# Two-layer encoder trunk: where the norms' squares products, the operand sums of the seven-product tiles and the last gate columns stand in the program's order

## The chip, the cores and the metric

The kernel runs on one core of one Trainium2 chip. The metric is the device time of one execution in microseconds (us). The kernel before the change took 2275.96 us in the median of three runs (2275.76 to 2279.22).

## The reference

One inference step of an encoder with two layers, for 1024 prompt frames and 32 sample frames (1056 columns in all, "T"), with a model width of 1024. Layer 0 mixes frames with a matrix-memory recurrence (mLSTM, 8 heads), layer 1 with windowed attention (16 query heads on 2 shared key and value heads). Behind each mixer stands a norm, then a gated feed-forward network (FFN) of width 2816, then another norm:

```
def layer_norm(x, g, b):
    mu = jnp.mean(x, -1, keepdims=True)
    var = jnp.mean(jnp.square(x - mu), -1, keepdims=True)
    return (x - mu) * lax.rsqrt(var + LN_EPS) * g + b

def swiglu(x, w_gu, w_down):
    g, u = jnp.split(x @ w_gu, 2, axis=-1)
    return (jax.nn.silu(g) * u) @ w_down

def trunk(x, ...):
    for layer in range(DEPTH):                 # DEPTH = 2
        if layer < N_A_LAYERS:                 # N_A_LAYERS = 1
            mix, C, n, m = mlstm_mixer(x, ...)
        else:
            k_sh, v_sh = x @ w_kv              # shared keys and values
            mix = swa_prompt(x, k_sh, v_sh, ...)
        x = layer_norm(DEEPNORM_ALPHA * x + mix, ln_g[layer, 0], ln_b[layer, 0])
        x = layer_norm(DEEPNORM_ALPHA * x + swiglu(x, w_gu[layer], w_down[layer]), ln_g[layer, 1], ln_b[layer, 1])
```

So there are four norms. They are numbered 0 (behind the mLSTM), 1 (behind the first FFN), 2 (behind attention) and 3 (behind the second FFN, the output).

## The kernel before

**Precision and products.** All is fp32. TensorE takes each operand as a high and a low half, and one "step" is three products: high by high (L358), high by low (L359), low by high (L360), in `gemm`. For weights, `Weights` loads a raw block `wr` (SyncE), ScalarE casts the high half `wh` (L198), and GpSimd or VectorE makes the low half `wl` (L200, raw minus high); some of these halves lie in borrowed buffers called `ex`. For activations the halves lie in `sx`.

**What sets the order.** The program is written out in one order by a planner, `Weave`. A task is a Python generator; each number that it yields is a span of planned TensorE time. After each step of three products `gemm` calls `tick` with the planned length of that step (0.34 for 264 columns), and tasks whose span has run out issue their next piece there. `drain` runs a task to its end, or until a condition holds, at once. Each engine works off its instructions in the order in which they were issued, so a piece that is issued earlier stands ahead of everything issued later on its engine, ready or not.

**A norm.** Columns are worked on in four quarters of 264. While the projection ahead of a norm makes its eight output tiles for a quarter (for norms 0 and 2 in `mixer_out`, L1098 adds the residual; for norm 1 in the down projection, L1466 does), `norm_tail` adds up the tiles (L595 and L597, VectorE). Then it launches `ln_task` for that quarter, which runs while TensorE goes on with the next quarter or with what follows the norm. Its pieces: the mean's product on TensorE (L417); centring in four instructions (L422, VectorE); the squares on ScalarE (L424); their additions (L426, two instructions on VectorE or GpSimd, and L429, VectorE); then, `yield y[3]` after L429 was issued, the squares product `pv` on TensorE (L433); the reciprocal root on ScalarE and VectorE (L437 to L443); the scaling (L447, VectorE), gain and bias (L457 on ScalarE, L455 on VectorE), the high half (L463) and the low half (L469) of the result. `y` comes from the table `LN_PACE`.

**The FFN.** The 22 pairs of a gate and an up tile (128 rows each) are made one after the other. The first two (`FIRST = 2`) are plain (`up_plain`): one set for the column half c = 0 (quarters 0 and 1), then the same for c = 1 (quarters 2 and 3), whose fourth quarter waits for the fourth `ln_task`. The other 20 take a scheme with seven products of half-size blocks in place of eight (`up_tile`), with four extra operands t1 to t4, which are sums of blocks of the activations. `sums(c)` makes them for one column half: per operand and pair of rows, an addition or subtraction on VectorE (L1248 for t3, L1250 for t2, L1252 for t4, L1254 for t1), the high half on ScalarE (L1238), the low half on VectorE or GpSimd in turn (L1235), one operand per 2.6 planned us; t1 waits until the plain tiles of that half are through. `sums(0)` is launched behind the first three quarters' norm tasks, `sums(1)` behind the fourth's. Before the first seven-product tile, `summed` drains both where they are not done. L1216 is the plain tiles' gating on VectorE.

**Behind norm 1** come the key and value projections of layer 1 (`k_group`, `v_group`), the queries (`q_group`: ScalarE copies at L1541 and L1542, low halves on VectorE at L1543 and L1546), and the attention, which starts with the scores' product (L1630) and its reader on VectorE (L1636).

**Gates.** In layer 0 the mLSTM's gates are worked out per group of 384, 384 and 288 frames by `gate_task`; `gates` makes them (L766 among its last rows is ScalarE's exponential), `gate_columns` transposes three pieces on TensorE (L781), each copied out of PSUM by ScalarE (L782, two PSUM banks in turn), and after the third group a small product brings the decays into columns (L793). `yield 3.0` stands between the third group's gates and its columns.

Of the kernel before, what the change touches and what calls it, by code (L numbers as in the profile page):

```python
# [52 lines left out]
    ((4.0, 1.2, 1.0, 3.6, 1.0, 1.4, 0.9), (3.8, 0.7, 0.8, 4.2, 0.8, 1.4, 1.0)),  # L53
    ((4.2, 0.9, 1.1, 4.4, 1.0, 1.4, 0.8), (4.2, 0.7, 0.9, 4.2, 0.8, 1.4, 0.8)),
)

RUSH = (3.2, 0.8, 0.6, 2.8, 0.8, 1.0, 0.6)

# [3 lines left out]
N4 = T // 4  # L62
# [176 lines left out]
def kernel(ctx: ExitStack, tc: tile.TileContext, A, O):  # L239
# [155 lines left out]

    QUARTERS = [(group(g), (g % 2, slice(0, N4))) for g in range(4)]

    def ln_task(z_, lps, grp, li, last, final):
        cols, (c, zs) = grp
        w = cols.stop - cols.start  # L400

        rush = final and grp is QUARTERS[2]
        y = RUSH if rush else LN_PACE[li & 1][last]
        acc = z_[:, 0:2, c, zs]
        sq = [acc] + [z_[:, 2 + 2 * i : 4 + 2 * i, c, zs] for i in range(3)]
        rs, r2 = z_[:, 8, c, zs], z_[:, 9, c, zs]
        n = KT // 2

        def z2(kk):
            return ACT[:, 2 * kk : 2 * kk + 2, cols]  # L410

        def s2(i, kk):
            return SX[:, i, 2 * kk : 2 * kk + 2, cols]

        yield y[0]
        pm = new(lps, "ln", [P, 512], bufs=3 if li & 1 else 2)[:, :w]
        nc.tensor.matmul(pm, onesm[:], acc[:, 0, :], start=True, stop=True)  # L417
        yield y[1]
        for s in range(n + 2):
            if s < n:  # L420

                nc.vector.tensor_sub(z2(s), pm.unsqueeze(1).broadcast_to([P, 2, w]), z2(s))  # L422
            if 1 <= s <= n:
                nc.scalar.activation(sq[s - 1], z2(s - 1), AF.Square)  # L424
            if s >= 3:
                (nc.gpsimd if rush or not (last or s & 1) else nc.vector).tensor_add(acc, acc, sq[s - 2])  # L426
            yield y[2]
        if not rush:
            nc.vector.tensor_add(acc[:, 0], acc[:, 0], acc[:, 1])  # L429
        yield y[3]  # L430
        pv = new(lps, "ln", [P, 512], bufs=3 if li & 1 else 2)[:, :w]
        for i in range(1 + rush):
            nc.tensor.matmul(pv, onesm[:], acc[:, i, :], start=(i == 0), stop=(i == rush))  # L433
        yield y[4]

        if not li & 1:
            nc.scalar.preload_act_table_set("natural_log_exp_and_others")  # L437
        nc.scalar.activation(rs, pv, AF.Ln, bias=eps_ln[:])
        nc.scalar.activation(rs, rs, AF.Exp, scale=-0.5)
        nc.scalar.activation(r2, rs, AF.Square, scale=0.5 ** 0.5)  # L440
        yield y[5]
        nc.vector.scalar_tensor_tensor(r2, pv, eps_ln[:], r2, op0=ALU.add, op1=ALU.mult)
        nc.vector.scalar_tensor_tensor(rs, r2, 1.5, rs, op0=ALU.subtract, op1=ALU.mult)  # L443
        for s in range(n + 3):
            if s < n:
                eng = nc.gpsimd if rush and s & 1 else nc.vector
                eng.tensor_mul(z2(s), z2(s), rs.unsqueeze(1).broadcast_to([P, 2, w]))  # L447
            kk = s - 1
            if 0 <= kk < n:
                for k in (2 * kk, 2 * kk + 1):  # L450
                    z, gk, bk = ACT[:, k, cols], lng[:, li, k : k + 1], lnb[:, li, k : k + 1]
                    if rush and k & 1:
                        nc.gpsimd.tensor_scalar(z, z, gk, bk, op0=ALU.mult, op1=ALU.add)
                    elif li & 1 and last and k & 1:
                        nc.vector.tensor_scalar(z, z, gk, bk, op0=ALU.mult, op1=ALU.add)  # L455
                    else:
                        nc.scalar.activation(z, z, AF.Identity, scale=gk, bias=bk)  # L457
            kk = s - 2
            if 0 <= kk < n:
                if final:  # L460
                    nc.sync.dma_start(O["y"][:, 2 * kk : 2 * kk + 2, cols], z2(kk))
                else:
                    nc.scalar.copy(s2(0, kk), z2(kk))  # L463
                    if li == 1:
                        nc.scalar.dma_start(scr[:, 2 * kk : 2 * kk + 2, cols], z2(kk))
            kk = s - 3
            if kk >= 0 and not final:
                eng = nc.gpsimd if kk & 1 else nc.vector
                eng.tensor_sub(s2(1, kk), z2(kk), s2(0, kk).bitcast(F32))  # L469
            yield y[6]  # L470
# [186 lines left out]
    cols = [pa.tile([P, 3, 96], F32, name=f"cols{g}") for g in range(3)]  # L657
# [126 lines left out]
    def gate_task():  # L784
        for g in range(3):
            while mst["v"] < 3 * g + 3:
                yield 0.5
            yield from gates(g)
        yield 3.0
        gate_columns(*late.pop())  # L790
        pd = new(psa, "T", [P, 512], bufs=2)
        for j in range(PAIRS):
            nc.tensor.matmul(pd[:, 9 * j : 9 * j + 9], sel[:, j, :], dec[:], start=True, stop=True)  # L793
        nc.vector.tensor_copy(dcol[:], pd[:, : 9 * PAIRS].rearrange("p (j c) -> p j c", j=PAIRS))
# [318 lines left out]
    def ffn(layer, li, tasks, lx, final):  # L1113
# [107 lines left out]
        def sums(c):  # L1221


            def x(k, par):
                return ACT[:, k : k + 2, group(2 * c + par)]

            todo = [(o, k) for k in range(0, H, 2) for o in ("t3", "t2", "t4")] + [("t1", k) for k in range(0, H, 2)]
            bufs = [Z[:, i : i + 2, c, :] for i in (7, 9)]

            def halve(s, low):  # L1230
                if 0 <= s < len(todo):
                    o, k = todo[s]
                    d = X[o](c)[:, :, k : k + 2, :]
                    if low:
                        (nc.vector if s & 1 else nc.gpsimd).tensor_sub(d[:, 1], bufs[s % 2], d[:, 0].bitcast(F32))  # L1235
                        made.append((c, o))
                    else:
                        nc.scalar.copy(d[:, 0], bufs[s % 2])  # L1238

            for s in range(len(todo) + 2):  # L1240
                halve(s - 2, True)
                if s < len(todo):
                    o, k = todo[s]
                    while o == "t1" and not plain[c]:
                        yield 0.3
                    t, before = bufs[s % 2], bufs[(s - 1) % 2]
                    if o == "t3":
                        nc.vector.tensor_sub(t, x(k + H, 1), x(k, 1))  # L1248
                    elif o == "t2":
                        nc.vector.tensor_add(t, before, x(k, 0))  # L1250
                    elif o == "t4":
                        nc.vector.tensor_sub(t, x(k + H, 0), before)  # L1252
                    else:
                        nc.vector.tensor_sub(t, x(k, 1), x(k, 0))  # L1254
                halve(s - 1, False)
                yield 2.6
# [650 lines left out]
```

## Time and profile before

| what | us |
|---|---|
| median of three runs | 2275.96 |
| lowest, highest run | 2275.76, 2279.22 |
| profiled execution, first to last instruction (span) | 2273.4 |
| TensorE busy, of that span | 2196.6 |
| VectorE busy | 1475.9 |
| ScalarE busy | 1013.4 |
| GpSimd busy | 1131.3 |
| mean granted clock of TensorE | 0.990 |

The profiled execution is a single one; what is known of it is its span of 2273.4 us, which is 2.6 us less than the median of the runs. Engines are written PE (TensorE), DVE (VectorE), ACT (ScalarE), POOL (GpSimd) and SP (SyncE, whose queue issues the transfers). A row of a timeline reads: start, duration, engine, line of the program, operation, output and inputs by their names, shapes, number of instructions in the row, and in brackets the idle time of the engine ahead of it with what ended that. L200 is line 200 of the program before; in the changed program the same lines stand 2 to 7 further down (L200 becomes L202, L358 to L360 become L360 to L362, L422, L426, L429 and L433 become L426, L430, L433 and L437, L442 and L447 become L447 and L452, L595 and L597 become L600 and L602, L781 and L793 become L786 and L798, L1098 becomes L1103, L1216 becomes L1221, L1235 and L1238 become L1242 and L1245, L1248, L1250 and L1252 become L1255, L1257 and L1259).

### The profile page before, as it was taken

How to read it: one execution, taken by the hardware profiler on the slowest of the kernel's cores; microseconds unless marked ns; L12 is line 12 of the kernel's file. 1: busy time of each engine (PE TensorE's matmuls, PEld its weight loads, DVE VectorE, ACT ScalarE, POOL GpSimd, SP SyncE). 2: the span in 40 equal slices, each digit the busy share in tenths (PEclk: the TensorE clock that was granted, in tenths of full speed). 3: DMA queues.
4: the chain of work that ended last, by engine and by line, in shares of the span. 5: the costliest groups of instructions: out<-in, count | busy, mean ns of one | idle time of the engine just before them, and what ended most of it. 6: DMA issues, size and time to landing. Idle time of an engine off the chain costs nothing. (4 is left out here: it accounts for less than half of the span.)

```text
span 2273.4 us, 44264 instructions
## 1 busy us (share of the span) xinstructions
PE 2196.6 (97%) x17166; PEld 2152.2 (95%) x17166; DVE 1475.9 (65%) x2771; ACT 1013.4 (45%) x2281; POOL 1131.3 (50%) x1040
## 2 busy tenths in 40 slices
PE   8999999999999999999998999999999999999997
PEld 8889989999999999999998998889999999999997
DVE  4354466777666665466667779877666666466657
ACT  3343355455434444322246788656444444421124
POOL 2443333226666666554326776633666666554422
PEclk9999999999999999999999999999999999999998
DMA  4221212302444434697524211411344344397712
GB/s 147 69 57 52 56 42 71 118 21 73 143 152 152 152 134 151 206 329 245 162 77 139 85 60 44 142 57 47 119 146 142 136 150 161 123 337 252 250 54 77
DMA packets 167298, 291.54 MB, mean 128 GB/s; under 512 B 16496, under 2 KB 123048, under 8 KB 167088
## 3 DMA queue, kind: packets, MB, share of 16 engines
q1 hardware_dynamic: 162736, 284.38, 37.5%
q10 hardware_dynamic: 4352, 4.33, 0.5%
q8 instruction: 135, 2.21, 0.4%
q14 instruction: 75, 0.61, 0.1%
HBM read 203.89 MB, written 82.94 MB: 126 GB/s over the span
## 5 line engine op out<-in xcount | busy, mean ns | idle before, releaser
L200 POOL TENSOR_TENSOR wl_s<-wr,wh_s 128x512 fp32r<-128x512 f32 x224 | 316.5, 1433 | 237.9 <-ACT wh_s L198 166.8
L358 PE MATMUL d<-sx,wh 128*128 128x264 f32 (+2 forms) x1068 | 342.3, 320 | 9.6 <-ACT sx L388 7.5
L360 PE MATMUL d<-sx,wl 128*128 128x264 f32 (+2 forms) x1068 | 327.8, 307 | 2.9 <-DVE wl L200 2.2
L359 PE MATMUL d<-sx,wh 128*128 128x264 f32 (+2 forms) x1068 | 327.7, 307 | 0.5 <-DVE sx L389 0.3
L198 ACT CAST wh_s<-wr 128x512 fp32r<-128x512 f32 x224 | 135.4, 617 | 316.3 <-DVE wr L175 288.6
L358 PE MATMUL A<-sx,wh_s 128*128 128x264 f32 x896 | 254.6, 284 | 2.7 <-ACT z L1299 2.7
L359 PE MATMUL A<-sx,wh_s 128*128 128x264 f32 x896 | 254.2, 284 | 0.0
L360 PE MATMUL A<-sx,wl_s 128*128 128x264 f32 x896 | 254.0, 283 | 0.0
L200 POOL TENSOR_TENSOR wl<-wr,wh 128x512 fp32r<-128x512 f32 (+2 forms) x103 | 141.1, 1376 | 220.8 <-ACT wh L198 190.3
L358 PEld LDWEIGHTS d<-sx,wh 128*128 128x128 f32 x1068 | 204.2, 191 | 14.5 <-ACT sx L388 7.8
L360 PEld LDWEIGHTS d<-sx,wl 128*128 128x128 f32 x1068 | 203.8, 191 | 3.9 <-DVE wl L200 2.8
L359 PEld LDWEIGHTS d<-sx,wh 128*128 128x128 f32 x1068 | 204.6, 192 | 2.0 <-DVE sx L389 1.0
L200 POOL TENSOR_TENSOR wl_a<-wr,wh_a 128x512 fp32r<-128x512 f32 x112 | 170.0, 1524 | 51.3 <-ACT wh_a L198 42.3
L358 PE MATMUL d<-sx,ex 128*128 128x264 f32 x624 | 182.1, 292 | 0.8 <-ACT sx L388 0.8
L360 PE MATMUL d<-sx,ex 128*128 128x264 f32 x624 | 178.8, 286 | 2.9 <-DVE ex L200 2.9
L359 PE MATMUL d<-sx,ex 128*128 128x264 f32 x624 | 178.8, 287 | 0.8 <-DVE sx L389 0.7
L358 PEld LDWEIGHTS A<-sx,wh_s 128*128 128x128 f32 x896 | 168.4, 188 | 3.1 <-ACT z L1299 3.1
L360 PEld LDWEIGHTS A<-sx,wl_s 128*128 128x128 f32 x896 | 168.9, 188 | 0.0
L359 PEld LDWEIGHTS A<-sx,wh_s 128*128 128x128 f32 x896 | 168.4, 188 | 0.0
L1171 POOL TENSOR_TENSOR z<-z 128x528 fp32r<-128x528 f32 x76 | 104.9, 1381 | 106.1 <-ACT z L1170 51.3
L1654 POOL TENSOR_SCALAR s<-s,st 128x256 f32<-128x256 f32 (+1 forms) x144 | 123.8, 871 | 56.8 <-DVE st L1652 43.3
L1170 ACT CAST z<-z 128x528 fp32r<-128x528 f32 x136 | 85.9, 631 | 97.3 <-DVE z L1183 47.4
(324 smaller groups left out, 7378.3 us busy)
## 6 DMA issues: line engine op xcount, KB each, us to landing
wr<-in_gu SPq DMA_DIRECT2D x96, 512.0 KB, 4.3
hs_x<-z SPq DMA_DIRECT2D x72, 528.0 KB, 2.6
hs_t<-z SPq DMA_DIRECT2D x64, 528.0 KB, 4.8
sx<-hs_x SPq DMA_DIRECT2D x112, 264.0 KB, 5.7
sx<-hs_t SPq DMA_DIRECT2D x64, 264.0 KB, 6.1
ex<-hs_t SPq DMA_DIRECT2D x64, 264.0 KB, 6.1
wr<-in_dn SPq DMA_DIRECT2D x32, 512.0 KB, 5.2
ex<-hs_x SPq DMA_DIRECT2D x32, 264.0 KB, 6.1
```

The costliest lines, as they stand in the source:

```text
L198: self.nc.scalar.copy(hi, r)
L200: eng.tensor_sub(lo, r, hi.bitcast(F32))
L358: nc.tensor.matmul(out, ah, bh, start=start and k == 0, stop=False, **kw)
L359: nc.tensor.matmul(out, ah, bl, start=False, stop=False, **kw)
L360: nc.tensor.matmul(out, al, bh, start=False, stop=stop and k == last, **kw)
L1170: nc.scalar.copy(hi.bitcast(F32R), buf(s))
L1171: eng.tensor_sub(lo.bitcast(F32R), buf(s), hi)
L1654: nc.gpsimd.tensor_scalar_mul(p[:R, h, lo:256], p[:R, h, lo:256], st[:R, 2, h : h + 1])
```

## The change

Four places, all of them order only: no instruction's work changes.

```diff
+LN_LAG = {(1, 2): 1.2, (1, 3): 1.4, (2, 0): 7.0}
...
+    spread_out = set()
...
     def ln_task(z_, lps, grp, li, last, final):
...
-        yield y[3]
+        yield y[3] + LN_LAG.get((li, cols.start // N4), 0.0)
         pv = new(lps, "ln", [P, 512], bufs=3 if li & 1 else 2)[:, :w]
         for i in range(1 + rush):
             nc.tensor.matmul(pv, onesm[:], acc[:, i, :], start=(i == 0), stop=(i == rush))
+        spread_out.add((li, cols.start // N4))
         yield y[4]
...
     def gate_task():
...
             yield from gates(g)
-        yield 3.0
+        yield 5.0
         gate_columns(*late.pop())
...
         def sums(c):
...
             bufs = [Z[:, i : i + 2, c, :] for i in (7, 9)]
+            while (li - 1, 3) not in spread_out:
+                yield 0.3
```

In `ln_task` the squares product of norm 1's quarters two and three (counted from 0), and of norm 2's quarter 0, is issued 1.2, 1.4 and 7.0 planned us later, and with it all that follows in that task. In `gate_task` the last group's columns are issued 2.0 later. In `sums`, nothing is issued until the squares product of the fourth quarter of the norm ahead of this FFN (norm 0 or 2) has been; this touches the FFNs of both layers. On TensorE only the gates' small products and three squares products change places (three steps later for norm 1's two, twenty for norm 2's); SyncE's order is the same.

VectorE's order in the first FFN, around the additions of norm 0's fourth quarter; `act` is the activations, `ln` the mean in PSUM, `z` the norm's and the sums' buffers. Before:

```order
L1248 TENSOR_TENSOR z_4629<-act 128x2x264
L1250 TENSOR_TENSOR z_4629<-z_4629,act 128x2x264
L422 TENSOR_TENSOR act<-ln_5990,act 128x2x264 x2
L1252 TENSOR_TENSOR z_4629<-act,z_4629 128x2x264
L200 TENSOR_TENSOR wl_1_6016<-wr_5064,wh_1_6015 128x512
L422 TENSOR_TENSOR act<-ln_5990,act 128x2x264 x2
L426 TENSOR_TENSOR z_4629<-z_4629 128x2x264 x2
L1235 TENSOR_TENSOR ex_4625<-z_4629,ex_4625 128x2x264
L1248 TENSOR_TENSOR z_4629<-act 128x2x264
L1216 TENSOR_TENSOR z_4629<-z_4629,d_6011 128x264
L426 TENSOR_TENSOR z_4629<-z_4629 128x2x264
L429 TENSOR_TENSOR z_4629<-z_4629 128x264
```

and of the change:

```order
L426 TENSOR_TENSOR act<-ln_5987,act 128x2x264 x2
L202 TENSOR_TENSOR wl_1_6010<-wr_5064,wh_1_6009 128x512
L426 TENSOR_TENSOR act<-ln_5987,act 128x2x264 x2
L430 TENSOR_TENSOR z_4629<-z_4629 128x2x264 x2
L1221 TENSOR_TENSOR z_4629<-z_4629,d_6005 128x264
L430 TENSOR_TENSOR z_4629<-z_4629 128x2x264
L433 TENSOR_TENSOR z_4629<-z_4629 128x264
L1221 TENSOR_TENSOR z_4629<-z_4629,d_6048 128x264
L202 TENSOR_TENSOR wl_1_6081<-wr_5708,wh_1_6080 128x512
L1255 TENSOR_TENSOR z_4629<-act 128x2x264
```

Five operations of the sums (L1248 twice, L1250, L1252, L1235) are gone from between the centring and the last addition; the first of them (now L1255) stands behind the addition, a gating and a weight's low half. The same holds in the second FFN.

VectorE's order at norm 2's first quarter, whose last addition of squares is L429 before and L433 now; `ex` here are weight halves, `d` the projection's PSUM banks. Before:

```order
L595 TENSOR_TENSOR z_17803<-act 128x2x264
L200 TENSOR_TENSOR ex_17799<-wr_17853,ex_17799 128x512
L429 TENSOR_TENSOR z_17803<-z_17803 128x264
L1098 SCALAR_TENSOR_TENSOR act<-act,d_17965 128x264
L200 TENSOR_TENSOR ex_17799<-wr_17888,ex_17799 128x512
L1098 SCALAR_TENSOR_TENSOR act<-act,d_17998 128x264
L595 TENSOR_TENSOR z_17803<-z_17803,act 128x2x264
L442 SCALAR_TENSOR_TENSOR z_17803<-ln_18015,eps_ln,z_17803 128x264
L443 SCALAR_TENSOR_TENSOR z_17803<-z_17803 128x264
L447 TENSOR_TENSOR act<-act,z_17803 128x2x264 x2
```

and of the change:

```order
L600 TENSOR_TENSOR z_17803<-act 128x2x264
L202 TENSOR_TENSOR ex_17799<-wr_17853,ex_17799 128x512
L433 TENSOR_TENSOR z_17803<-z_17803 128x264
L1103 SCALAR_TENSOR_TENSOR act<-act,d_17965 128x264
L202 TENSOR_TENSOR ex_17799<-wr_17888,ex_17799 128x512
L1103 SCALAR_TENSOR_TENSOR act<-act,d_17998 128x264
L600 TENSOR_TENSOR z_17803<-z_17803,act 128x2x264
L1103 SCALAR_TENSOR_TENSOR act<-act,d_18029 128x264
L1103 SCALAR_TENSOR_TENSOR act<-act,d_18055 128x264
L600 TENSOR_TENSOR z_17803<-z_17803,act 128x2x264
L602 TENSOR_TENSOR z_17803<-z_17803 128x264
L447 SCALAR_TENSOR_TENSOR z_17803<-ln_18087,eps_ln,z_17803 128x264
```

The rows up to the addition stay where they were; the norm's tail (L442 before, L447 now) stands behind two more residuals and the next quarter's last additions.

TensorE's order at the last group's gate columns; `g` is the gates, `d` a projection. Before:

```order
L360 MATMUL d_863<-sx,wl_0_412 128x288
L781 MATMUL T_870<-ident,g_49_769 128x96
L781 MATMUL T_873<-ident,g_49_769 128x96
L781 MATMUL T_876<-ident,g_49_769 32x96
L793 MATMUL T_879<-dec,sel 128x9 x4
L358 MATMUL d_863<-sx,wh_0_411 128x288
```

and of the change:

```order
L362 MATMUL d_863<-sx,wl_1_744 128x288
L786 MATMUL T_885<-ident,g_49_769 128x96
L786 MATMUL T_888<-ident,g_49_769 128x96
L786 MATMUL T_891<-ident,g_49_769 32x96
L798 MATMUL T_894<-dec,sel 128x9 x4
L360 MATMUL d_863<-sx,wh_1_743 128x288
```

The four rows stand within the second half of the projection's eight steps (`wl_1`) where they stood in the first (`wl_0`), five steps later.

## The prediction

> **What bounds the kernel now.** I read the page first, then the table of waits on TensorE, then TensorE's timeline at those waits, the windows around them with their granted clock, and last VectorE's timeline at the same places.
>
> ```profile
> span 2273.4 us, 44264 instructions
> PE 2196.6 (97%) x17166; PEld 2152.2 (95%) x17166; DVE 1475.9 (65%) x2771; ACT 1013.4 (45%) x2281; POOL 1131.3 (50%) x1040
> ```
>
> TensorE is busy for 97% of the span, so time is won only where it stands still or runs slowly. In the table of its waits (us in total, times, longest) one line belongs to what the change moves:
>
> ```profile
> PE ln L433 <- DVE z L429: 13.5, 5, 5.6
> ```
>
> L433 is the norms' squares product. It waits five times, 13.5 us in all, for L429, the last addition of squares on VectorE. On TensorE's timeline the five are (the bracket is the idle time before the row):
>
> ```profile
> 517.50 0.71 PE L433 MATMUL ln<-z,onesm 128*128 128x264 f32 x2 [2.89 <-DVE z L429]
> ...
> 1202.60 0.68 PE L433 MATMUL ln<-z,onesm 128*128 128x264 f32 x2 [0.94 <-DVE z L429]
> ...
> 1222.70 0.68 PE L433 MATMUL ln<-z,onesm 128*128 128x264 f32 x2 [1.12 <-DVE z L429]
> ...
> 1491.36 1.25 PE L433 MATMUL ln<-z,onesm 128*128 128x264 f32 x2 [5.57 <-DVE z L429]
> ...
> 1567.73 1.25 PE L433 MATMUL ln<-z,onesm 128*128 128x264 f32 x2 [3.03 <-DVE z L429]
> ```
>
> They are the fourth quarter of norm 0, quarters three and four of norm 1, the first quarter of norm 2 and the fourth of norm 2. A wait can cost more than its length. In the windows view the columns are length, PE busy (count), granted clock, DMA share, GB/s:
>
> ```profile
> 515.72:519.13 3.41, 1.63 (x11) 1.00 0.00 0
> 1485.10:1488.52 3.42, 0.69 (x6) 1.00 0.15 59
> ...
> 1491.93:1495.34 3.41, 3.41 (x16) 0.50 0.82 256
> 1495.34:1498.75 3.41, 3.41 (x30) 1.00 0.13 52
> 1563.61:1567.02 3.41, 1.09 (x9) 1.00 0.00 0
> 1567.02:1570.44 3.42, 2.71 (x10) 0.50 0.00 0
> 1570.44:1573.85 3.41, 3.41 (x18) 0.50 0.48 154
> ...
> 78.81:82.22 3.41, 3.41 (x15) 0.50 0.00 0
> 82.22:85.64 3.42, 3.42 (x22) 1.00 0.00 0
> ```
>
> Behind a window with 0.69 or 1.09 us of work the clock is halved for the next; behind one with 1.63 it isn't. A full window holds 30 products (0.114 us each, 0.34 per step of three), a halved one 16: 14 x 0.114 = 1.6 us lost.
>
> The Trainium skill (TensorE: Matmul & The Clock Gate, The HAM clock gate) says that the clock is halved after an idle window of about 3.4 us, and that the windows run freely. The second half agrees with these equal 3.41 us windows; the first is too mild, since 1.09 us of work did not prevent it here. By its letter the 3.03 us wait would have cost no clock.
>
> **The change, part by part.**
>
> *Gate columns.* Three transposes and the small products behind them go five steps later on TensorE. Now:
>
> ```profile
> 76.21 0.30 PE L781 MATMUL T<-ident,g 96*128 96x96 f32 x1 [0.28 <-ACT g L766]
> 77.55 0.26 PE L781 MATMUL T<-ident,g 96*32 96x96 f32 x1 [1.03 <-ACT cols L782]
> ```
>
> The second of these rows is bound by ScalarE, which copies the first column set out of the way only behind the gates' exponentials. 1.31 us of waits; five steps later (about 2 us) ScalarE is through with these, and what stays is the wait for its copy alone, as in an earlier group:
>
> ```profile
> 70.49 0.30 PE L781 MATMUL T<-ident,g 96*128 96x96 f32 x1 [0.25 <-ACT cols L782]
> ```
>
> Gain 1.31 - 0.25 = 1.06. The window at 78.81 is halved too: 15 products instead of 22 are 7 x 3.42 / 22 = 1.1 us; I count 0.9 of it, since a shorter pause may still trip it. **Gates: -2.0** (bounds -0.5 and -2.4). The columns' reader comes a whole head pair later.
>
> *Sums behind the fourth squares product (norms 0 and 2).* VectorE in front of L429 today:
>
> ```profile
> 503.15 1.81 DVE L1248 TENSOR_TENSOR z<-act 128x528 f32<-128x528 f32 x1
> 505.00 0.71 DVE L1250 TENSOR_TENSOR z<-z,act 128x528 f32<-128x528 f32 x1
> ...
> 507.13 0.71 DVE L1252 TENSOR_TENSOR z<-act,z 128x528 f32<-128x528 f32 x1 [0.20 <-POOL ex L1235]
> ...
> 512.49 1.81 DVE L1235 TENSOR_TENSOR ex<-z,ex 128x528 fp32r<-128x528 f32 x1
> 514.33 1.69 DVE L1248 TENSOR_TENSOR z<-act 128x528 f32<-128x528 f32 x1
> ...
> 517.01 0.43 DVE L429 TENSOR_TENSOR z<-z 128x264 f32<-128x264 f32 x1
> ```
>
> All five operations above L429 go behind it: 1.81 + 0.71 + 0.71 + 1.81 + 1.69 = 6.7 us. Of these the 0.71, 1.81 and 1.69 stand straight in its way, so that L429 ends at 517.44 - 4.2 = 513.2. TensorE arrives at 514.6: the 2.89 us go.
>
> But the 6.7 us come back while the plain tiles run, and there VectorE has little room:
>
> ```profile
> PE d L360 <- DVE wl L200: 1.5, 1, 1.5
> PE d L359 <- POOL sx L469: 0.2, 1, 0.2
> ...
> 515.00:556.50 41.50, 37.32 (x300) 36.76 (x301) 34.53 (x45) 25.36 (x48) 22.25 (x15) 1.00 0.20 64
> ...
> 539.98 0.71 DVE L1252 TENSOR_TENSOR z<-act,z 128x528 f32<-128x528 f32 x1 [2.52 <-ACT wh L198]
> 540.60 1.76 DVE L200 TENSOR_TENSOR wl<-wr,wh 128x512 fp32r<-128x512 f32 x1
> ```
>
> The first two rows are TensorE's waits from 500 to 560 us besides L433. In the window's row the third busy figure is VectorE's: 34.5 of 41.5 us. The seven-product tiles begin at 556.5, and come 2.9 us sooner if the wait goes. From 513.2 to then there are 40.4 us, for 34.5 - 2.4 (done by then) + 6.7 = 38.8. The idle time shrinks from 7.0 to 1.6 us, while single waits like the 2.52 above stay. Already now the L200 behind it, the low half of a weight, is late: it ends at 542.36, and it is what TensorE waits 1.5 us for; it waits another 0.2 for a fourth-quarter operand. Both places lie behind the sums' old one, so these 1.7 us are made up anew. Afterwards it will wait for such halves between 0.2 (all fits) and 3.4 us (two waits of 2.5 less the 1.6); I take 2.5, near the upper end, since hardly any idle time is left. Norm 0: 2.89 + 1.7 - 2.5 = **-2.1** (0 to -4.4).
>
> Norm 2 has the same order:
>
> ```profile
> PE d L360 <- DVE wl L200: 0.2, 1, 0.2
> ```
>
> Beside its 3.03 us TensorE waits 0.2 there for a weight half, and the clock is halved: 12 of 30 products missing in one window (1.4 us), about 1.0 in the part of the other behind 1567.73. 3.03 + 0.2 + 2.4 - 2.5 = **-3.1** (-0.8 to -5.5).
>
> A rule of the Trainium skill speaks against this part: a Vector instruction with two SBUF inputs contends with GpSimd's reads, and the one that comes second is blocked for the whole instruction (SBUF — State Buffer, Who interferes with whom). L1248's eight instructions agree in their spread, shortest, median and longest in ns:
>
> ```profile
> L1248 DVE TENSOR_TENSOR z<-act x8: 696/1201/1821, 503.1 to 1595.9; 128x528 f32<-128x528 f32 x8
> ```
>
> If closer packing made all five moved operations 1.8 us, they would be 9.0 instead of 6.7, and each layer's gain 2.3 us less; the sum below would be 2269.5.
>
> *Norm 2, first quarter, 7 later.* The product goes 20 steps later; TensorE goes on with the output projection meanwhile. What it meets is VectorE's queue, unchanged up to L429:
>
> ```profile
> 1489.21 1.75 DVE L200 TENSOR_TENSOR ex<-wr,ex 128x512 fp32r<-128x512 f32 x1
> 1490.88 0.42 DVE L429 TENSOR_TENSOR z<-z 128x264 f32<-128x264 f32 x1
> ...
> 1491.56 0.68 DVE L200 TENSOR_TENSOR ex<-wr,ex 128x512 fp32r<-128x512 f32 x1
> ```
>
> From 1485.8 the sixth tile's second half takes 4 steps (to 1487.2), the seventh's first half 4 more (1488.5); its second half needs the low weights that L200 finishes at 1490.96. So 5.57 becomes about 2.3 us. L429 is done at 1491.3 and the product now comes near 1495: no wait. 5.57 - 2.3 = 3.3, and the halved window 1.6, and 0.3 for the product itself at full speed; less a third of 1.6, because 2.3 us can trip the clock too: **-4.7** (-2.5 to -7.5, the upper end without that wait). Its tail falls beside quarter two's additions, whose product is not among today's five waits; I count nothing for it.
>
> *Norm 1, quarters three and four, 1.2 and 1.4 later.* Quarter three buys nothing: behind its product today stands
>
> ```profile
> 1204.03 0.41 PE L358 MATMUL d<-sx,wh 128*128 128x384 f32 x1 [0.74 <-DVE act L1466]
> ...
> 1203.46 0.76 DVE L1466 TENSOR_TENSOR act<-act,d 128x264 f32<-128x264 f32 x2
> ```
>
> The key projection waits for a PSUM bank that L1466 reads, to 1204.03 with or without the norm. The two waits become one, from 1202.60 - 0.94 = 1201.66 to 1204.03, 2.4 us, which can trip the clock (1.6 x 0.4 = 0.6). The product comes three steps of 384 columns (0.5 each) behind that, at 1205.6, 3.0 us later than today; of its own two, one at least no longer lies inside a wait (0.2 to 0.3). Quarter four saves up to 1.12 us, but 10 us later TensorE stands still in any case:
>
> ```profile
> 1239.45 0.58 PE L1630 MATMUL psS<-KH,Q 128*128 128x256 f32 x1 [5.51 <-DVE st L1636]
> ```
>
> L1636 is queued on VectorE behind the whole tail of quarter four and the query copies, so a gain before it vanishes in this wait, and a later tail can lengthen it. I take no change there (bounds -1 to +1.5). **Norm 1: +0.8** in all (0.6 + 0.2; -1 to +3).
>
> Other queues: SyncE's transfers keep their order; ScalarE and GpSimd only see the sums' casts and low halves later.
>
> **Sum.** -2.0 - 2.1 - 3.1 - 4.7 + 0.8 = -11.1 us. Against the profiled span that is 2273.4 - 11.1 = 2262.3; the median of the runs, 2275.96, lies 2.6 above that span, so 2264.9.
>
> **Rivals.**
>
> *The sums give nothing (A).* VectorE's crowding eats both layers' gain: 2275.96 - 2.0 - 4.7 + 0.8 = 2270.1. For it speak the 1.6 us of idle time left; against it that weight halves behind the product come some 4 us sooner.
>
> *Later norms lengthen the wait for scores (B).* The 3.0 us of quarter three reach L1636, and 1.6 of clock: 2264.9 + 4.6 = 2269.5. Against it: VectorE still idles for ScalarE's query copies on the way to L1636, which is slack that a later tail can use up first:
>
> ```profile
> 1237.74 0.55 DVE L1543 SCALAR_TENSOR_TENSOR Q<-d,Q 64x384 fp32r<-64x384 f32 x1 [0.55 <-ACT Q L1542]
> ```
>
> *Slower (C).* The crowding goes further: VectorE runs 38.8 us and both 2.5 us waits, and each moved operation at 1.8 (2.3 more): 46.1 for 40.4, some 5.7 us of TensorE waits per layer, which are short enough to trip the clock twice each (3.2). Against 2.89 + 1.7 and 3.03 + 0.2 + 2.4 today, that is 4.3 and 3.3 worse: -2.0 - 4.7 + 0.8 + 7.6 = +1.7, and with quarter three's 4.6 reaching the scores too, +6.3: 2282.3. It decides from about 5 us of such waits per layer ((2 x 5 + 6.4) - 10.2 makes up the other parts' 5.9). VectorE's 7.0 us of idle time today speaks against it.
>
> *The change does little (D).* Weight halves late everywhere, quarter one included: 2274.
>
> **Numbers.** Forecast 0.57, A 0.18, B 0.12, D 0.08, C 0.05. Its own range is 2259 to 2269; with A and B and the open clock windows 2258.5 to 2273. A measurement tells about 0.2% (4.6 us) from no change. Faster by more: forecast, A, B, less some tails: 0.83. Same: 0.12. Slower: 0.05.
>
> **What would show it.** In the changed profile: the squares product with under 2 us of waits in all; no halved clock behind norm 2's first quarter, or one behind a 2.3 us wait for a low weight half; more waits for such halves (1 to 3 us) in both plain stretches; the key projection waiting some 2.4 us for L1466's successor; the wait for scores still 5 to 6 us. I am wrong if the seven-product tiles begin by waiting for their sums, or the score wait grows past 8 us.

## The result, and the profile after

The change made no difference that can be told: 2274.84 us in the median of 13 runs (2271.10 to 2279.71) against 2276.30 for the kernel before on the same chips (13 runs, 2272.35 to 2279.22), a ratio of 0.9994 with a 95% interval of 0.9987 to 1.0002. The forecast was 2264.9 us in a range of 2258.5 to 2273.0, which the result lies above. The profiled execution of the changed kernel takes 2272.2 us, 1.2 less than the one before. The head of its page:

```profile
span 2272.2 us, 44264 instructions
...
PE 2195.4 (97%) x17166; PEld 2147.8 (95%) x17166; DVE 1485.2 (65%) x2771; ACT 1014.9 (45%) x2281; POOL 1132.5 (50%) x1040
```

VectorE does the same 2771 instructions as before and takes 9.3 us longer over them (1475.9 before). TensorE's waits in the changed kernel (us in total, times, longest):

```profile
PE psS L1637 <- DVE st L1643: 7.5, 2, 6.6
...
PE d L362 <- DVE ex L202: 5.4, 6, 1.5
PE d L362 <- DVE wl L202: 4.6, 4, 1.7
PE d L361 <- DVE sx L474: 2.6, 2, 1.3
...
PE d L360 <- DVE act L1473: 2.4, 1, 2.4
```

The 13.5 us for the norms' squares are gone, all five waits. In their place stand waits for weight halves (L202), for the fourth quarter's operands (L474), for the key projection's PSUM bank (L1473, 0.7 before) and for the scores (L1643, 6.5 before).

Where the time went is seen best by the start of the same TensorE instruction in the two traces. The table gives, at places between the stages that the change touches, how much later (+) or earlier (-) it starts in the changed kernel; each is a difference of two timeline rows.

| reached in the kernel before, us | after minus before, us | step | what lies in the step | forecast of the step |
|---|---|---|---|---|
| 56 | -0.4 | -0.4 | start | |
| 382 | -2.1 | -1.7 | gate columns | -2.0 |
| 608 | +0.3 | +2.4 | norm 0's fourth quarter, plain tiles, first seven-product tiles | -2.1 |
| 1184 | +1.3 | +1.0 | rest of the first FFN | |
| 1240 | +4.3 | +3.0 | norm 1 to the first scores | +0.8 |
| 1465 | +3.5 | -0.8 | attention | |
| 1517 | -2.4 | -5.9 | norm 2's first quarter | -4.7 |
| 1643 | -0.7 | +1.7 | norm 2's fourth quarter, plain tiles, first seven-product tiles | -3.1 |
| end | -1.2 | -0.5 | rest | |

So the lag at norm 2 and the gates gave what they should, and the sums and norm 1 took it back. In the first FFN the squares product itself starts 5.2 us earlier than before (at 512.32 instead of 517.50, 2.1 of it the lead that TensorE had at 382), and within 45 us all of it is lost again.

Each step is one pair of traces, and a halved clock window more or less is 1.6 us. The traces of the runs below show how far a stage moves when its part of the program is as before: -2.1 to +3.1 us against the trace before from 56 to 382, -0.8 to +0.5 from 382 to 608, -0.1 to +1.6 from 1184 to 1240, -1.4 to 0 from 1517 to 1643. The last one says that the trace before was itself slow there, so the +1.7 is rather too little.

### The profile page after: what moved, and what is told of

Read it like the earlier page. It is cut to its first block, busy times and chain, and to the rows that moved or that the text cites. A ratio compares the mean times of both kernels' runs of the same rounds, so it can differ in the third digit from the quotient of the medians.

```text
span 2272.2 us, 44264 instructions
## 1 busy us (share of the span) xinstructions
PE 2195.4 (97%) x17166; PEld 2147.8 (95%) x17166; DVE 1485.2 (65%) x2771; ACT 1014.9 (45%) x2281; POOL 1132.5 (50%) x1040
## 5 line engine op out<-in xcount | busy, mean ns | idle before, releaser
L202 POOL TENSOR_TENSOR wl_s<-wr,wh_s 128x512 fp32r<-128x512 f32 x224 | 316.6, 1433 | 239.1 <-ACT wh_s L200 176.6
L202 POOL TENSOR_TENSOR wl<-wr,wh 128x512 fp32r<-128x512 f32 (+2 forms) x103 | 141.3, 1378 | 226.8 <-ACT wh L200 201.7
L202 POOL TENSOR_TENSOR wl_a<-wr,wh_a 128x512 fp32r<-128x512 f32 x112 | 169.3, 1518 | 48.7 <-ACT wh_a L200 41.9
L360 PE MATMUL A<-ex,wh_s 128*128 128x264 f32 x448 | 127.7, 285 | 1.3 <-ACT z L1289 1.3
```

Source lines behind the costliest of these rows:

```text
L202: eng.tensor_sub(lo, r, hi.bitcast(F32))
L360: nc.tensor.matmul(out, ah, bh, start=start and k == 0, stop=False, **kw)
```

## The experiments

All are timed against the kernel before on the same chip. Theory T says that each part does in time what the table shows. Its rivals are P, the prediction's own sum, with the table put down to chance clock windows, and Z, that no part does anything.

**The parts alone.** The sums' wait without the rest:

```diff
-LN_LAG = {(1, 2): 1.2, (1, 3): 1.4, (2, 0): 7.0}
+LN_LAG = {}
...
-        yield 5.0
+        yield 3.0
         gate_columns(*late.pop())
```

> Only the sums' wait for the fourth squares product is kept; the three lags and the gates' pause are as before. Theory T (the parts add up as the two traces' offsets show): the 2.9 and 3.0 us waits for the squares go, but VectorE is full behind them, TensorE waits for weight halves and fourth-quarter operands instead: +2.5 us in the first FFN, +1.7 in the second, together about +4 (ratio 1.002). Rival P (the prediction's sum, and the trace after shows chance clock windows): -2.1 and -3.1, together -5 (0.998). Rival Z (each part is worth nothing): within 1 us of the kernel before.

Measured: 1.0022 (1.0013 to 1.0032), +5.0 us. The first FFN loses 2.6 and the second 1.7 in the trace (382 to 608 and 1517 to 1643), with the same waits as in the changed kernel. T holds; P, which had -5, falls.

Norm 1 alone (`LN_LAG = {(1, 2): 1.2, (1, 3): 1.4}`, no wait of the sums, gates at 3.0):

> Only norm 1's squares products of quarters three and four are later (1.2 and 1.4). T: the key projection waits 2.4 us, quarter three's tail comes 4 us later on VectorE, is mixed into quarter four's centring, and the wait for the scores is longer, not shorter: +3 to +3.7 us (1.0015). Rival P: +0.8 us (1.0004). Rival Z: within 1 us.

Measured: 1.0009 (1.0000 to 1.0018), +2.0 us, between T and P. The interval (0 to +4.1 us) holds both, so this run does not tell them apart.

Norm 2's first quarter alone (`LN_LAG = {(2, 0): 7.0}`):

> Only norm 2's first squares product is later (7.0). T: TensorE's 5.6 us wait becomes one of 1.5 us for a low weight half, the halved clock behind it goes or is shorter: -5.5 to -6 us (0.9975), in the trace between 1485 and 1502. Rival P: -4.7 (0.998). Rival Z: within 1 us.

Measured: 0.9976 (0.9966 to 0.9986), -5.5 us. That is T's figure, but P's -4.7 lies in the interval too; Z falls.

The same with the gates' `yield 5.0`:

> The gates' later columns and norm 2's later first squares product, without the sums' wait and without norm 1's lags. T: -2.1 for the gates (0.3 to 1.3 us of waits and one halved clock window) and -5.9 for norm 2, together -8 (0.9965). Rival P: -2.0 - 4.7 = -6.7 (0.997). Rival Z: within 1 us.

Measured: 0.9971 (0.9959 to 0.9982), -6.6 us. That is P's figure (-6.7), and T's -8 lies in the interval. The gates add about -1.1, less than the -1.7 of the table, with intervals that overlap widely. The four parts add up to 5.0 + 2.0 - 5.5 - 1.1 = +0.4 us against -1.4 measured for the whole (-3.0 to +0.5), so nothing speaks for an interaction between them.

**Norm 1's two quarters.** Each of the two lags alone:

```diff
-LN_LAG = {(1, 2): 1.2, (1, 3): 1.4}
+LN_LAG = {(1, 2): 1.2}      # or {(1, 3): 1.4}
```

> Only the third quarter (number 2 from 0) of norm 1 has its squares product 1.2 later. Theory T2: this one is the loss: its tail falls among the fourth quarter's centring, which ends some 3 us later, and the wait for the scores takes it over: +2 to +4 us between 1200 and 1245 in the trace (ratio 1.001). Rival U (the fourth quarter's lag makes the loss, its tail being the one in front of the scores): within 1 us.

> Only the fourth quarter (number 3 from 0) of norm 1 has its squares product 1.4 later. T2: the 1.1 us wait for the squares goes and the wait for the scores grows by as much, no net change within 1 us (1.000). Rival U: +2 to +4 us (1.001).

Measured: 1.0017 (1.0009 to 1.0026) for quarter three, +3.9 us, and 1.0000 (0.9991 to 1.0009) for quarter four. T2 holds. TensorE's waits from 1195 to 1250 us with quarter three's lag alone (L1635, L1641 and L1471 are here what L1637, L1643 and L1473 are in the changed kernel):

```profile
PE psS L1635 <- DVE st L1641: 5.3, 1, 5.3
PE ln L437 <- DVE z L433: 2.8, 1, 2.8
PE d L360 <- DVE act L1471: 2.4, 1, 2.4
```

and with quarter four's alone:

```profile
PE psS L1635 <- DVE st L1641: 6.6, 1, 6.6
PE ln L437 <- DVE z L433: 1.0, 1, 1.0
PE d L360 <- DVE act L1471: 0.7, 1, 0.7
```

Quarter three's lag makes one wait of 2.4 out of 0.94 and 0.74, and lets quarter four's squares come later (2.8 instead of 1.1). Quarter four's lag takes 1.1 us away there (the 1.0 that is left is quarter three's) and gives it back at the scores, 6.6 instead of 5.5.

**The sums: is VectorE too full?** With the wait alone, all low halves of the sums are put on GpSimd, which in the changed kernel hardly works for ten us behind the squares product:

```diff
-                        (nc.vector if s & 1 else nc.gpsimd).tensor_sub(d[:, 1], ...)
+                        nc.gpsimd.tensor_sub(d[:, 1], ...)
```

> The sums' wait alone, as in the run of it, but all low halves of the sums are made on GpSimd, none on VectorE. Theory C (VectorE's crowding behind the squares product is what eats the gain): with some 1.7 us of every second low half taken off VectorE, TensorE's waits for weight halves in the first FFN's plain tiles fall from 3.0 to under 1 us and those for the fourth quarter's operands from 1.8 to under 1; the first FFN gains about 2 us on the kernel before where it lost 2.7, the second about 2.5 where it lost 1.6; ratio near 0.998. Rival Q (the chain from the squares product to the fourth quarter's operands is just as long, and GpSimd's queue becomes the late one): the waits stay in other rows, ratio 1.001 to 1.003.

The same line changed in the kernel before, without the wait:

> The kernel before with one thing changed: all low halves of the sums on GpSimd, and no wait for the sums. Theory C: the low half of 1.8 us that stands ahead of the last addition of squares goes, so the squares' wait in the first FFN falls from 2.9 to about 1.1 us and in the second from 3.0 to about 1.2, and the waits for weight halves shrink as well: -3 to -6 us (0.998). Rival Q: GpSimd's queue is late in its place (weight halves or operand halves made there): no gain, 0.999 to 1.001.

Measured: 1.0071 (1.0059 to 1.0083) and 1.0059 (1.0046 to 1.0072): 16 and 13 us slower. Theory C as put there falls, and the loss is far above Q's figures too. The window from 525 to 556 us (length, then busy time of PE, PEld, DVE, ACT, POOL with counts, granted clock, DMA share, GB/s), in the kernel before, in the changed one, and with the wait and the low halves on GpSimd:

```profile
525.00:556.00 31.00, 29.33 (x238) 28.83 (x237) 24.26 (x31) 16.41 (x34) 18.70 (x12) 1.00 0.21 69
...
525.00:556.00 31.00, 26.14 (x202) 24.71 (x201) 30.73 (x32) 13.51 (x26) 21.02 (x13) 1.00 0.17 52
...
525.00:556.00 31.00, 24.75 (x168) 23.64 (x168) 26.32 (x24) 13.41 (x26) 28.99 (x19) 0.89 0.16 52
```

GpSimd is busy 29.0 of 31 us, at up to 1.8 us for one low half, and it makes some of the weight halves and operands too. VectorE's load fell from 30.7 to 26.3, and TensorE did less than in the changed kernel (168 products against 202), in part at a halved clock. So these two runs neither show nor rule out that VectorE is too full, since they only move the lateness into another queue.

**The sums: other places and paces.** First a pause in place of the wait (`while (li - 1, 3) not in spread_out` is gone): the sums begin as before and stand still from the fourth quarter's mean product to its squares product. The gates' and norm 2's first quarter's edits are in it too:

```diff
+        centring.add((li, cols.start // N4))
         pm = new(lps, "ln", [P, 512], bufs=3 if li & 1 else 2)[:, :w]
...
             for s in range(len(todo) + 2):
+                while (li - 1, 3) in centring - spread_out:
+                    yield 0.3
```

> The run with the gates' columns and norm 2's first squares product later, and beside it another form of the sums' wait: they begin as in the kernel before and stand still only from the mean's product of the norm's fourth quarter to its squares product, so that two or three of their operations stay in front. Theory V (both VectorE's order in the norm's tail and its fullness behind it make the waits, by the amount of work that is moved): the waits for the squares stay gone, those for weight halves in the first FFN's plain tiles fall from 3.0 to 1 to 2 us, the operands' 1.8 falls to about 1; the first FFN then costs between -1.5 and +1 us against the kernel before, the second the same; ratio 0.996 to 0.9975, no worse than 0.9971. Rival W (any sums behind the squares product cost the 2.5 and 1.7): 0.999.

Measured: 0.9994 (0.9985 to 1.0003), against 0.9971 without any pause of the sums. Two operations fewer behind the product gained nothing: in the first FFN's plain tiles TensorE waits 2.8 us for weight halves and 2.6 for operands, and 0.6 for the squares. V falls; W is what happened: the stretches from 382 to 608 and from 1517 to 1643 cost 2.5 and 1.4 us.

Then the wait alone, but until the norm's tail has been issued (the line `spread_out.add(...)` moved to the end of `ln_task`):

> The sums' wait alone, but longer: until the last low half of the fourth quarter's norm has been issued, some 9 us later. V: the fourth quarter's operands are no longer late (TensorE's waits for them 1.8 to 0.2 us or less), but weight halves and the sums themselves are much later: 3.0 becomes 5 us or more and the first seven-product tile waits for its sums; +4 us or more in each FFN, ratio 1.004 to 1.008. Rival X (only the collision with the norm's tail costs): the loss goes, ratio 0.998 to 1.000.

Measured: 1.0037 (1.0024 to 1.0049). TensorE's waits from 505 to 560 us:

```profile
PE B L360 <- DVE z L1221: 4.7, 1, 4.7
PE d L362 <- DVE wl L202: 1.3, 1, 1.3
PE d L360 <- DVE z L1221: 0.9, 1, 0.9
```

The operands' waits are gone, so it was the sums in front of the norm's low halves that made them late. But X, which had the loss go with them, falls. V is right on the late seven-product tiles and nearly on the time, not on its 5 us of waits for weight halves (1.3). What was gained waits at the end, for a gating that stands behind the sums on VectorE:

```profile
553.71 0.69 DVE L1242 TENSOR_TENSOR ex<-z,ex 128x528 fp32r<-128x528 f32 x1
554.44 1.68 DVE L1261 TENSOR_TENSOR z<-act 128x528 f32<-128x528 f32 x1
556.05 0.75 DVE L1221 TENSOR_TENSOR z<-z,d 128x264 f32<-128x264 f32 x2
```

Last, the two waits with a faster pace behind them, 1.5 planned us in place of 2.6 (for the first column half only; for both behind the tail):

```diff
-                yield 2.6
+                yield 1.5 if c == 0 else 2.6      # behind the tail: yield 1.5
```

> The sums' wait alone, and the first column half's sums then issued every 1.5 planned us instead of 2.6. In the trace of the change VectorE is busy for 62% and GpSimd for 2% of the ten us behind the squares product, and VectorE for 99% of the twenty from 531 on. Theory G (the idle slot right behind the squares product is what is lost; filled sooner, there is room): the weight-half waits of 3.0 us in the first FFN's plain tiles fall under 1.5, and the loss of 2.7 and 1.6 us falls to about 0; ratio 1.000. Theory H (the sums' casts stand behind the norm's reciprocal root on ScalarE, so VectorE's queue blocks on them whenever they are issued, and the tail comes later): the operands' waits grow from 1.8 to 3 us or more and the loss stays: ratio 1.002 or more.

> The sums' wait until the fourth norm's tail has been issued, and all sums then issued every 1.5 planned us instead of 2.6. With 2.6 the plain tiles ran nearly without waits, and TensorE paid 4.7 and 5.1 us before the seven-product tiles, for a gating that stood on VectorE behind the sums that were then made all at once. G: spread over the plain tiles they fit, that wait falls to 1 us or less, and each FFN gains 1 to 2.5 us on the kernel before; ratio 0.998 to 0.999. H (VectorE has no room for some 10 us more between the tail and the seven-product tiles, at any pace): the 4.7 us come back as waits for weight halves in the plain tiles; ratio 1.002 or more.

Measured: 1.0016 (1.0007 to 1.0025) and 1.0058 (1.0044 to 1.0072). G, which had no loss and a gain, falls both times. Sooner behind the product, the operands wait longer (3.1 us in all instead of 1.8), as H says, though the loss itself is no larger than with 2.6 and a little under H's figure; spread over the plain tiles, the 4.7 us come back there as waits for weight halves (4.3 for the low, 3.3 for the high ones). H's reason, no room on VectorE, is not what this last run shows: from 530 to 540 us VectorE is busy for 6.8 of ten there. VectorE, ScalarE and GpSimd wait for each other in turn over the sums, and the weights' casts stand behind the sums' casts on ScalarE.

**What is best.** Norm 2's first quarter with 4.0 instead of 7.0, and the gates:

> The run with the gates' columns and norm 2's first squares product later, with 4.0 in place of 7.0. Theory T: what is left there is the 1.5 us wait for a low weight half, which comes after eight steps; twelve steps are enough, so the same 1.5 us and -5.7 us between 1485 and 1502, ratio 0.997. Rival Y (the longer lag matters, since the squares are done only at 1491.3): a squares wait of 1 us or more comes back, ratio 0.998.

Measured: 0.9968 (0.9956 to 0.9980), 2268.13 us against 2275.52. T holds: no squares wait comes back, and the trace shows a wait of 2.0 us for the same weight half and -5.4 between 1485 and 1502. The whole gain of the change is in two of its four edits; without the sums' wait and norm 1's lags it beats both kernels, by 7.3 us the one before.

## Why the prediction was wrong

**Gates: right, as far as the runs can tell.** -2.0 forecast, -1.7 in the trace, about -1.1 timed. The new rows are those that were expected, the first two transposes in one go and 0.25 us for ScalarE's copy:

```profile
77.27 0.33 PE L786 MATMUL T<-ident,g 96*128 96x96 f32 x2
77.85 0.26 PE L786 MATMUL T<-ident,g 96*32 96x96 f32 x1 [0.25 <-ACT cols L787]
```

The -1.7 is a sum of two things, though. At 82 us TensorE has gained 2.8, and at 100 us it loses 1.9 in a wait for L860 that the trace before does not have: GpSimd starts that one's input 2.4 us after its queue is free, for a reason that the profile does not show. The same wait (2.0) stands in one run without the gates' edit, so it is not shown to come from the edit. From 56 to 382 the four traces with the edit lie at -1.7 to -2.8 and the ten others at -2.1 to +3.1, so that a single pair agreeing with -2.0 is partly luck.

**Norm 2's first quarter: right.** -4.7 forecast, -5.5 timed; the five traces with a lag there have -3.5 to -5.9 from 1465 to 1517, the small ones with a halved clock behind the wait. The step said that the 5.57 us wait becomes one of about 2.3 for a low weight half, the clock perhaps halved behind it:

```profile
1493.94 0.39 PE L362 MATMUL d<-sx,ex 128*128 128x264 f32 x1 [1.50 <-DVE ex L202]
```

and on VectorE:

```profile
1492.13 1.75 DVE L202 TENSOR_TENSOR ex<-wr,ex 128x512 fp32r<-128x512 f32 x1
1493.80 0.42 DVE L433 TENSOR_TENSOR z<-z 128x264 f32<-128x264 f32 x1
```

It is that half (it ends at 1493.88), 1.5 us here and 1.6 to 2.2 in the other runs with this lag.

**The sums: wrong, and this is the error that decided.** Forecast -5.2 us for both layers, timed alone +5.0. The other three parts were forecast at -5.9 together and timed at -4.6, so this one makes about the whole miss. Two steps of it failed. The first was "TensorE arrives at 514.6: the 2.89 us go", with a charge for weight halves alone. The wait for the squares does go, but what the squares serve is the fourth quarter's operands, and the step never asked when those come; it named one only for 0.2 us that it counted as won. The next rows late are these:

```profile
525.94 0.39 PE L361 MATMUL d<-sx,wh 128*128 128x264 f32 x1 [0.48 <-POOL sx L474]
...
528.24 0.39 PE L361 MATMUL d<-sx,wh 128*128 128x264 f32 x1 [1.31 <-DVE sx L474]
```

and on VectorE, in front of the low half that the second one waits for:

```profile
524.64 1.81 DVE L1259 TENSOR_TENSOR z<-act,z 128x528 f32<-128x528 f32 x1 [2.52 <-POOL ex L1242]
526.37 0.41 DVE L1221 TENSOR_TENSOR z<-z,d 128x264 f32<-128x264 f32 x1
526.71 1.48 DVE L474 TENSOR_TENSOR sx<-act,sx 128x528 fp32r<-128x528 f32 x1
```

A sum that used to stand in front of the squares now stands in front of the norm's result, first blocked for 2.5 us by its own buffer and then taking 1.8. Of 2.9 us won, 1.8 are paid there. That the sums' place does it is shown by the run with the sums behind the tail, where these waits vanish. The 2.5 us are a sum that waits until GpSimd has read one of the two buffers that all sums of a column half share; in the run with the pause that wait is 4.3 us. No run gives the sums a third buffer, so how much of the loss this makes stays open.

The second failing step was the room on VectorE. "34.5 - 2.4 (done by then) + 6.7 = 38.8" for 40.4 us took the window as one, and the moved operations at the durations of their old place. In the changed kernel VectorE works for 34.3 of these 40.4 us (513.2 to 553.6), so it was not too full in all. But the idle time lies at the front, where its queue could not use it, and the rest is full. The changed kernel, ten us each from 1.0 before the squares product on:

```profile
511.30:521.30 10.00, 10.00 (x83) 9.93 (x82) 6.20 (x10) 8.27 (x15) 0.23 (x1) 1.00 0.26 81
521.30:531.30 10.00, 8.21 (x66) 7.79 (x64) 7.34 (x8) 7.04 (x14) 8.39 (x6) 1.00 0.07 27
531.30:541.30 10.00, 8.72 (x69) 8.30 (x69) 9.93 (x11) 5.10 (x10) 6.20 (x5) 1.00 0.31 86
541.30:551.30 10.00, 8.21 (x66) 7.82 (x65) 9.93 (x10) 5.07 (x10) 7.38 (x5) 1.00 0.23 73
```

VectorE (third busy figure) has 6.2 and 7.3 of ten at first, GpSimd (fifth) 0.2, since both wait for ScalarE's reciprocal root and the casts queued behind it:

```profile
515.65 0.49 DVE L447 SCALAR_TENSOR_TENSOR z<-ln,eps_ln,z 128x264 f32<-128x264 f32 x1 [2.96 <-ACT z L445]
...
522.02 1.30 POOL L202 TENSOR_TENSOR wl<-wr,wh 128x512 fp32r<-128x512 f32 x1 [10.49 <-ACT wh L200]
```

Then VectorE has 9.9 of ten, twice. Forty us of the kernel before, from 512.5 on, hold the same 33.4 us of VectorE work, with the full stretch at the front:

```profile
512.50:522.50 10.00, 7.11 (x57) 6.84 (x56) 9.90 (x12) 6.31 (x11) 6.06 (x4) 1.00 0.18 62
522.50:532.50 10.00, 9.83 (x80) 9.54 (x78) 6.82 (x12) 9.69 (x19) 3.95 (x3) 1.00 0.15 56
532.50:542.50 10.00, 8.49 (x68) 8.28 (x68) 7.41 (x9) 4.71 (x10) 7.14 (x5) 1.00 0.16 53
542.50:552.50 10.00, 10.00 (x83) 10.00 (x84) 9.25 (x11) 4.44 (x9) 6.23 (x4) 1.00 0.35 107
```

Weight halves waited for: 3.0 us where 2.5 were forecast, so that term was nearly right. The sum was still wrong by 4.5 us in the first FFN: 1.8 for the operands, 0.7 for waits at the first seven-product tiles (2.1 after, 1.4 before), 0.5 for the weight halves, and 1.5 that are in no listed wait's length (below). In the second it was wrong by 4.8.

The durations did change as well. The prediction priced all five moved operations at 1.8 us, 2.3 us more per layer, and left it out of the sum. The groups of t4's sums and of the low halves, shortest, median and longest in ns, before:

```profile
L1252 DVE TENSOR_TENSOR z<-act,z x8: 707/708/1686, 507.1 to 1599.2; 128x528 f32<-128x528 f32 x8
...
L1235 DVE TENSOR_TENSOR ex<-z,ex x12: 695/701/1835, 512.5 to 1607.6; 128x528 fp32r<-128x528 f32 x12
```

and after:

```profile
L1259 DVE TENSOR_TENSOR z<-act,z x8: 695/1729/1814, 524.6 to 1598.5; 128x528 f32<-128x528 f32 x8
...
L1242 DVE TENSOR_TENSOR ex<-z,ex x12: 694/1640/1834, 528.1 to 1607.0; 128x528 fp32r<-128x528 f32 x12
```

The medians of these two groups went from 0.7 to 1.7 us; that of t1's sums fell from 1.3 to 0.7. Of all 48 VectorE instructions of the sums, 19 took over 1 us before and 24 after, and every one of these overlaps a GpSimd instruction by more than 0.35 us; of the shorter ones 9 of 29 and 8 of 24 do. This is the rule of the Trainium skill that the prediction weighed (SBUF — State Buffer, Who interferes with whom: a Vector instruction with two SBUF inputs contends with a GpSimd instruction that reads SBUF). The trace agrees in the long ones, though an overlap alone does not make an instruction long. The sums took 51.7 us of VectorE before and 56.8 after, five more at about 1 us each over both layers, near the 4.6 of the remark.

**Norm 1: within its range, but too small.** Forecast +0.8 (-1 to +3), in the trace +3.0, timed alone +2.0. The 2.4 us wait stands where it was forecast, the clock was halved behind it, and the product is three steps later:

```profile
1205.36 0.41 PE L360 MATMUL d<-sx,wh 128*128 128x384 f32 x1 [2.39 <-DVE act L1473]
...
1207.79 1.08 PE L437 MATMUL ln<-z,onesm 128*128 128x264 f32 x2
```

With both lags and no other edit the clock stayed full behind that wait, and the same stretch took +1.4. The failing step is "ScalarE and GpSimd only see the sums' casts and low halves later". Quarter three's tail is later too, and its low half (L474) now stands on GpSimd in front of weight halves that TensorE waits for:

```profile
1223.57 1.79 POOL L474 TENSOR_TENSOR sx<-act,sx 128x528 fp32r<-128x528 f32 x1
1225.33 7.11 POOL L202 TENSOR_TENSOR wl<-wr,wh 128x512 fp32r<-128x512 f32 x5
...
1227.10 0.44 PE L362 MATMUL d<-sx,wl 128*128 128x384 f32 x1 [1.08 <-POOL wl L202]
```

So the 1.12 us that quarter four's squares product no longer waits are paid here, and once more at the scores, 6.6 us instead of 5.5. That the scores take up what is won ahead of them was forecast.

**The rivals.** B had quarter three's tail lengthen the wait for scores; with quarter three's lag alone it is 5.3 us, and with quarter four's alone 6.6, so B is not what happened. C is nearest: it alone had the sums lose, and it named longer operations. It had each layer at waits of more than 5.7 us with two halved windows and a chance of 0.05, and its overfull VectorE is not in the trace (34.3 of 40.4 us). The runs put the sums' loss at +5.0 us, where C had +7.6. D's 2274 is the measured time by accident: its reason, weight halves late in norm 2's quarter one included, would have taken the gain that this quarter gave.

Of the signs that the prediction named, most came true: no squares wait, a 1.5 us wait for a low weight half at norm 2's first quarter, 3.0 and 1.7 us of such waits in the plain stretches, 2.4 at the key projection. They test the parts that were thought of, and what cost the time was not among them.

## What to carry to other kernels

When a wait is removed by moving work off the queue in front of it, follow the chain to its last consumer and the moved work to its new neighbours: here the 2.9 us wait for the squares went, and the sum that had made them late made the norm's result late instead. Room on an engine counts only where its queue can use it, so split a window of "idle" time at the waits inside it before adding work to it. Putting a waiting product later pays where its engine has other work that is ready and nobody is in a hurry for the product's result (norm 2's first quarter, with the output projection to go on with); that was so at one of the five waits only.

## What the runs showed of the hardware

**A short wait costs more than its row says.** At the 0.48 us wait above, the row ahead starts at 525.17 and the waiting one at 525.94, 0.77 us where 0.12 is usual, and the next 0.23 later instead of 0.12: 0.76 us lost for 0.48 listed. At the 1.31 us wait it is 526.65 to 528.24 and 0.23, 1.58 us, and at the 1.50 us wait 1492.15 to 1493.94 and 0.22, 1.77 us. So each of these waits costs about 0.27 us beyond its length. Of that 0.16 come from the listing, which counts idle time from the end of a row of 0.28 us where the next usually starts after 0.12, and the rest is the slower next row. From 500 to 596 us TensorE has 710 products in the changed kernel and 730 before; the 20 are 2.4 us, where the listed waits are 6.9 and 6.0 us. Of the 1.5 us between, four waits turned into eight explain 1.1.

**Whether a wait of 2 us halves the clock depends on where the clock's windows cut it.** Behind the wait for norm 2's weight half the clock stayed full in three runs (1.50, 1.62 and 1.99 us) and was halved for one window in two (2.02 and 2.23 us), so 1.99 and 2.02 came out differently. With norm 2's lag alone (2.02 us), the windows with their granted clock (the third figure from the right):

```profile
1494.95:1498.36 3.41, 1.48 (x12) 1.48 (x13) 3.41 (x6) 0.00 (x0) 1.33 (x1) 1.00 0.08 16
1498.36:1501.80 3.44, 3.44 (x19) 3.44 (x18) 1.14 (x3) 0.00 (x0) 0.00 (x0) 0.50 0.79 288
```

In every trace the clock changes lie a multiple of 3.413 us apart. The Trainium skill (TensorE: Matmul & The Clock Gate, The HAM clock gate) has the windows run freely, which agrees: how they cut a wait decides, and 1.6 us a window hang on it. On each trace's own grid, the window that holds most of this wait has 2.23, 1.97 and 1.62 us of listed TensorE work where the clock stayed full, and 1.48 and 1.18 where it was halved. Over all fifteen traces, a full-speed window with under 1.4 us of work was always followed by a halved one and one with over 2.4 never. Between these both happen, so the prediction's 1.63 us, which kept the clock up, is no limit: the halved window at 78.81 in the trace before follows one with 2.10 us. Single runs of one kernel spread over 7 to 9 us here (13 runs of each), which fits, though no run isolates that.
